# One z chunk and one o chunk of each layer as a 2x2 block product with seven products

## The chip, the core and the metric

The kernel runs on one core of a Trainium2 chip. The metric is the device time of one execution in microseconds (us). The core's engines work side by side, each from its own queue of instructions: PE (TensorE, matrix products into PSUM), DVE (VectorE, elementwise work), ACT (ScalarE, functions and copies), POOL (GpSimd) and SP (SyncE, which here only issues transfers). Semaphores hold an engine until what it needs is there.

## The reference

Two layers over 256 positions of width 2048, then a last RMSNorm. A layer normalises x, multiplies it with a wide input matrix, and splits the result: q and k (convolved), v, an output gate o, a gate z for the mLSTM heads, and xb and zb for a gated linear recurrence. Both mixers' results, each multiplied by silu of its z, go through an output matrix and are added to x.

```python
u = rms_norm(x, norm_g)
p = u @ w_in
qk, v, o, z_a, ig, fg, xb, z_b = jnp.split(p, SPLIT_AT, axis=-1)
...
h = mlstm_chunkwise(q, k, v, i_pre, log_f)
h = h * jax.nn.sigmoid(o.astype(f32)).reshape(b_, s_, H_A, DV_A)
...
y_a = h.astype(x.dtype) * jax.nn.silu(z_a)
...
y_b = rg_lru(xc.astype(f32), w_a, b_a, w_x, b_x, lam).astype(x.dtype) * jax.nn.silu(z_b)
return x + jnp.concatenate([y_a, y_b], axis=-1) @ w_out
```

All is float32. o and z are 2048 columns wide each; the kernel works them off in four chunks of 512 columns.

## The kernel before

**Units and halves.** A layer has four groups g of two heads and 512 channels. A group's input chunks are o, qk, v, xb, z and zb, 512 columns each, 2048 rows deep. The weights lie in memory as units of 128 x 2048 numbers (1 MB); a chunk is four units, a unit two halves. One half carries two row blocks of 128 rows; it is multiplied with both halves of the positions (two times 128), and each product is made of three: a float32 number is split into a rounded part H and a remainder L, and H*H, H*L and L*H are added up in PSUM. That makes 12 matmuls of 128x512 for a half (`mm_a`, line 315). The activations x are kept split as well, transposed, 128 rows a block (`x_s`).

**Splitting the weights.** A unit is loaded by SP into one of three buffers `raw` (`load_unit`, 259). `prepare` (286) splits a half: ACT casts it to wH (line 308), DVE subtracts to get wL (309; it shows as line 168, that of a helper). There are four pairs of buffers wH/wL. The main loop (1101) issues, for half n, first the split of half n + 3 (AHEAD), then the half's matmuls, then what follows them.

**The work behind a chunk.** When a chunk's last half is done, a post function takes its result out of PSUM: `o_post` (sigmoid), `v_post`, `qk_post` and `xb_post` (both swap to channel order over DRAM and back, then convolve; the names are tok, blk, moved, fr, ch), `z_post`, `zb_post`. The longer ones put a generator on the list `bg`; after each half `pump` runs these generators in order for a budget (1.05 us by their own estimates, or 2.6 when more than two are in the list). Where a step needs a key that isn't there yet, `require` runs the generators until it is. So the order in which instructions are issued comes from this loop; each engine's final order is made by the framework's scheduler, by that order and by when operands are ready. Lines made by hand with `order` fix single places.

**The sequence.** In group 0 it is o, qk, v, xb, zb, z, gate; in group 2, o, v, qk, then two output chunks of group 1, xb, two output chunks, z, gate, zb. A gate unit (`gate_half`, 739) makes the recurrence's two gates: 48 matmuls of 128x256 (line 753) into four banks ps_gt, each emptied by two sigmoids (758). It requires xb's convolution (`gate_before`, 873). Behind it `gate_post` (763) has ACT make exponentials (770), tanh (776) and a square root, and DVE the recurrence.

**PSUM.** The eight banks are two accumulators acc of two banks, and four auxiliary banks (two names, two buffers each; `aux`, 99) for ps_gt, ps_S, ps_n and a few others. The output chunks of groups 0 to 2 go through a buffer `stage` (891), from which POOL adds them to x in DRAM.

## Time and profile before

| what | us |
|---|---|
| median of the runs (1493.61 to 1494.64) | 1493.76 |
| span of the profiled execution, first to last instruction | 1491.3 |
| PE busy | 1481.6 |
| PE weight loads busy | 1241.1 |
| DVE busy | 1050.9 |
| ACT busy | 925.8 |
| POOL busy | 81.8 |

Moved in all are 345.66 MB, 232 GB/s on the mean. The profile comes from one execution; its durations are those of that execution, and what lies around the span (the start and the end of the program) is not in it. In the rows of the groups "xN" counts instructions, then come busy time in us, mean ns of one, and the idle time of the engine just ahead of them with what ended it. The chain of work that ended last is followed back from the last instruction, at each step to what released it.

### The profile page before, as it was taken

Reading aid. Unit: us, or ns where it says so; the run is one execution under the profiler, and the core shown is the slowest. Engines: PE = TensorE matmul, PEld = TensorE weight load, DVE = VectorE, ACT = ScalarE, POOL = GpSimd, SP = SyncE. Lnnn points to the kernel's source line nnn. Section 1 sums busy time; section 2 is a strip of 40 time slices with the busy share of each in tenths; the row PEclk is TensorE's granted clock in tenths of the full one; section 3 lists DMA queues with packets and bytes.
Section 4 is the critical chain, followed back from the end, with each engine's and each line's share of the span. In section 5 each row is a group of like instructions: output and inputs, shape, how many; then the busy total and the mean of one; then the engine's idle time right before and its main releaser. Section 6 shows DMA issues by size and latency. Waiting matters only on the chain.

```text
span 1491.3 us, 18541 instructions
## 1 busy us (share of the span) xinstructions
PE 1481.6 (99%) x6894; PEld 1241.1 (83%) x6894; DVE 1050.9 (70%) x1406; ACT 925.8 (62%) x1167; POOL 81.8 (5%) x154
## 2 busy tenths in 40 slices
PE   9999999999999999999999999999999999999997
PEld 8888888888888888888888888888888888888886
DVE  6778976675567855778867798765855678556785
ACT  7656864575565855658575667645755567555675
POOL 0010100000000000000000101000000000000002
PEclk9999999999999999999999999999999999999999
DMA  9866766866677666876886666568666777577783
GB/s 337 296 224 221 227 221 208 254 224 216 199 239 232 217 225 217 258 258 226 270 277 195 231 219 240 205 205 253 223 223 216 238 223 234 200 229 265 231 282 111
DMA packets 91370, 345.66 MB, mean 232 GB/s; under 512 B 9984, under 2 KB 30480, under 8 KB 69776
## 3 DMA queue, kind: packets, MB, share of 16 engines
q1 hardware_dynamic: 79472, 306.44, 60.2%
q0 software_dynamic: 9344, 33.58, 9.1%
q10 hardware_dynamic: 2464, 4.47, 0.8%
q8 instruction: 54, 0.88, 0.2%
q14 instruction: 36, 0.29, 0.0%
HBM read 307.20 MB, written 37.24 MB: 231 GB/s over the span
## 4 chain that ended last, share of the span: by engine, by line
PE 99%; ACT 0%; DVE 0%; issue 0%; ACTq 0%
PE acc L332 89%; PE ps_gt L753 3%; PE acc L345 1%; PE acc L995 1%; PE acc L994 1%; PE acc L996 1%; PE acc_x L995 0%; PE acc_x L994 0%; PE acc_x L996 0%; PE ps_blank L110 0%; PE ps_n L589 0%; PE ps_n L587 0%; PE ps_n L588 0%; PE ps_g L500 0%; PE ps_g L503 0%; PE ps_S L588 0%
## 5 line engine op out<-in xcount | busy, mean ns | idle before, releaser
L332 PE MATMUL acc<-wH,x_s 128*128 128x512 f32 x3008 | 930.0, 389 | 0.0
L168 DVE TENSOR_TENSOR wL<-raw,wH 128x1024 fp32r<-128x1024 f32 (+1 forms) x532 | 636.5, 1204 | 341.8 <-ACT wH L308 341.3
L308 ACT CAST wH<-raw 128x1024 fp32r<-128x1024 f32 (+1 forms) x532 | 548.0, 1037 | 398.5 <-PE acc L332 367.6
L332 PEld LDWEIGHTS acc<-wH,x_s 128*128 128x128 f32 x3008 | 564.6, 188 | 116.9
L332 PE MATMUL acc<-wL,x_s 128*128 128x512 f32 x1504 | 583.9, 389 | 0.0
L332 PEld LDWEIGHTS acc<-wL,x_s 128*128 128x128 f32 x1504 | 282.3, 188 | 58.1
L332 PE MATMUL acc<-wH,yaH 128*128 128x512 f32 x224 | 87.4, 390 | 0.0
L332 PE MATMUL acc<-wH,ybL 128*128 128x512 f32 x224 | 87.3, 390 | 0.0
L332 PE MATMUL acc<-wH,yaL 128*128 128x512 f32 x224 | 87.2, 389 | 0.0
L332 PE MATMUL acc<-wL,ybH 128*128 128x512 f32 x224 | 87.2, 389 | 0.0
L332 PE MATMUL acc<-wH,ybH 128*128 128x512 f32 x224 | 87.2, 389 | 0.0
L332 PE MATMUL acc<-wL,yaH 128*128 128x512 f32 x224 | 87.2, 389 | 0.0
L332 PEld LDWEIGHTS acc<-wH,ybL 128*128 128x128 f32 x224 | 42.0, 188 | 9.1 <-DVE ybL L168 0.3
L332 PEld LDWEIGHTS acc<-wH,yaL 128*128 128x128 f32 x224 | 42.1, 188 | 9.0
L332 PEld LDWEIGHTS acc<-wH,ybH 128*128 128x128 f32 x224 | 42.1, 188 | 8.5
L332 PEld LDWEIGHTS acc<-wL,ybH 128*128 128x128 f32 x224 | 42.0, 188 | 8.5
L332 PEld LDWEIGHTS acc<-wL,yaH 128*128 128x128 f32 x224 | 42.1, 188 | 8.4
L332 PEld LDWEIGHTS acc<-wH,yaH 128*128 128x128 f32 x224 | 42.0, 188 | 8.2
L446 DVE STREAM_TRANSPOSE blk<-tok 128x1024 f32<-128x1024 f32 x33 | 40.8, 1237 | 11.0 <-ACT tok L436 11.0
L436 ACT ACTIVATE tok<-acc,rstd 128x512 f32<-128x512 f32 x46 | 29.1, 684 | 30.6 <-PE acc L332 30.6
L450 POOL DMA_DIRECT2D fr<-moved x34 | 18.9, 556 | 506.5 <-DMA moved<-blk 260.1
L892 ACT COPY stage<-acc 128x1024 f32<-128x1024 f32 x24 | 24.4, 1017 | 35.5 <-PE acc L332 35.3
(209 smaller groups left out, 1308.5 us busy)
## 6 DMA issues: line engine op xcount, KB each, us to landing
raw<-in_ws_dram SPq DMA_DIRECT2D x168, 1024.0 KB, 5.1
raw<-in_ws_dram SPq DMA_DIRECT2D x190, 512.0 KB, 4.9
fr<-moved POOLq DMA_DIRECT2D x34, 512.0 KB, 6.0
moved<-blk SPq DMA_DIRECT2D x132, 128.0 KB, 2.6
x_d<-stage POOLq DMA_DIRECT2D x24, 512.0 KB, 5.4
x_d<-x_acc ACTq DMA_DIRECT2D x8, 512.0 KB, 8.4
x_acc<-x_d SPq DMA_DIRECT2D x8, 512.0 KB, 4.4
xp<-in_xt_dram SPq DMA_DIRECT2D x8, 256.0 KB, 7.2
```

The lines of the kernel that those rows point to most:

```text
L168: return V.tensor_tensor(out=o, in0=a, in1=b, op=op)
L308: st["wH"] = S.copy(out=H[:, o], in_=r[:, o])
L332: st["mm"] = PE.matmul(o, a_[:, kt, P * t : P * t + P], W[:, k], start=b, stop=z)
L345: PE.matmul(ps[:, ct, T * part : 2 * T], W[:, k, P * ct : P * ct + P], moving, start=first and k == 0 and part == 0, stop=last and k == 3 ...
L436: S.activation(out=by_block(tok, t), in_=acc[:, t, :].rearrange("p (c m j) -> p c m j", c=4, m=4), func=AF.Copy, scale=rstd[:, t : t + 1])
L446: V.transpose(out=blk.rearrange("p m n -> p (m n)"), in_=tok.rearrange("p m c t j -> p (m c t j)"))
L450: back.dma_start(out=fr.rearrange("p a c t i -> p a (c t i)"), in_=moved)
L753: PE.matmul(o, W[:, ib, jl], xs[:, ib, a, :], start=j == 0 and i == 0 and W is Hv and a == 0, stop=i == 1 and W is Lv, skip_group_check=True)
L892: S.copy(out=stage, in_=ps)
L994: PE.matmul(o, yH[:, kt, tsl], Hv[:, k, cs], start=start and k == 0, stop=False)
L995: PE.matmul(o, yH[:, kt, tsl], Lv[:, k, cs], start=False, stop=False)
L996: PE.matmul(o, yL[:, kt, tsl], Hv[:, k, cs], start=False, stop=stop and k == 1)
```

## The change

The z chunk of group 2 and the o chunk of group 3 (`PAIR`) leave the sequence. With x as 2x2 blocks (two halves of the positions, two halves of the 2048 rows) and the weights as 2x2 blocks (two halves of the rows, two chunks), the product of both is made from seven block products in place of eight, each from sums or differences of blocks (the scheme known as Strassen's in Winograd's form).

- `block_halves` gives 28 halves as 14 pairs per layer: four phases of 4, 4, 2 and 4 pairs, two products at a time (one at a time in the third), in the two new PSUM banks bank0 and bank1. Such a half has two row blocks but only one half of the positions: 6 matmuls. Where a product needs a sum of weight blocks, DVE adds the raw blocks ahead of the split, 4, 12, 0 and 4 times in the four phases.
- A pair loads one unit of two pieces of 512 KB; a pair of the second phase two.
- `block_sums`, a generator, makes the four sums S1 to S4 of x blocks and their H and L parts, in buffers that share their place with x_acc (now two tiles, xa0 and xa1).
- The 14 pairs are spread evenly from the v chunk of group 0 to the place of z in group 2, directly ahead of that group's gate.
- After each phase the banks are emptied into `res`; after the last the results go to `o_post` and `z_post` (o from a generator that waits for group 2's recurrence, with the sign turned).
- The auxiliary banks have one buffer each (two in place of four).
- Smaller: nb goes into E, Pt shares the place of ch, the gate weights have one buffer; qk's generator waits for o's sigmoid too; the first output chunk of group 2 requires it ahead of its use of `stage`.

```diff
+PAIR = (("z", NG - 2), ("o", NG - 1))
...
     def aux(name):
         st["aux"] = 1 - st["aux"]
-        return psum.tile([P, 512], F32, tag=f"aux{st['aux']}", name=name, bufs=2)
+        return psum.tile([P, 512], F32, tag=f"aux{st['aux']}", name=name)
+
+    def bank(i, name):
+        return psum.tile([P, 512], F32, tag=f"bank{i}", name=name)
...
+        elif "pieces" in ld:
+            for i, (u, o) in enumerate(ld["pieces"]):
+                nc.sync.dma_start(out=raw[:, 1024 * i : 1024 * i + 1024], in_=ws[u][:, o : o + 1024])
...
+        if "sum" in hf:
+            r = hf["sum"]()
...
-        nb = small.tile([P, 2, T], F32, tag="nb", name="nb", bufs=1)
+        E = small.tile([P, 2, 384], F32, tag="E", name="E", bufs=1)
...
-            while ("E", l, g) not in st or ("v", l, g) not in st:
+            while any((k, l, g) not in st for k in ("E", "v", "so")):
...
+                if g == NG - 2 and c == 0:
+                    require(("so", l, g + 1))
...
+    def block_sums(l):
+        sums = st["sums", l] = [act.tile([P, 2, 8, P], F32R, tag=f"xa{i}", name=f"sums{i}") for i in range(2)]
...
+        def made(i, key, terms):
+            to = sums[i]
+            for k in (0, 4):
+                ks = slice(k, k + 4)
+                two = [work.tile([P, 4, P], F32, tag=tag, name="sum_t") for tag in ("tok", "blk")]
+                for a in range(2):
+                    terms(two, a, k, ks)
+                tt_(two[0], two[0], two[1], ALU.add)
+                S.copy(out=to[:, 0, ks], in_=two[0])
+                tt_(to[:, 1, ks], two[0], to.bitcast(F32)[:, 0, ks], ALU.subtract)
+                yield 2.4
+            st[key, l] = True
...
+    def block_halves(l):
...
+                for k in range(2):
+                    aH, aL = A(2 * kp + k)
+                    s_, e_ = kp == 0 and k == 0, kp == k_last and k == 1
+                    PE.matmul(box[b], aH, Hv[:, k], start=s_, stop=False)
+                    PE.matmul(box[b], aH, Lv[:, k], start=False, stop=False)
+                    PE.matmul(box[b], aL, Hv[:, k], start=False, stop=e_)
...
+        def after4():
+            r = st["res", l]
+            top = act.tile([P, 2, 512], F32, tag="stage", name="top")
+            tt_(top[:, 0], r[:, 2], box[0], ALU.add)
+            add(r[:, 1], box[1])
+            add(r[:, 2], box[1])
...
+            bg.append(gen())
+            z_post(l, g0, r)
+
+        pairs = []
+        for kp in range(4):
+            u = load(piece(0, 0, kp), piece(0, 1, kp))
+            pairs.append([half([u], lambda u=u: half_of(u, 0), plain(0, 0), 0, kp),
+                          half([u], lambda u=u: add(half_of(u, 1), half_of(u, 0)), summed(0), 1, kp, "S1",
+                               after=after1 if kp == 3 else None)])
+        for kp in range(4):
+            u, w = load(piece(0, 0, kp), piece(0, 1, kp)), load(piece(1, 1, kp), piece(1, 0, kp))
+            pairs.append([half([u, w], lambda u=u, w=w: add(half_of(w, 0), add(half_of(u, 1), half_of(u, 0))),
+                               summed(1), 0, kp, "S2"),
+                          half([w], lambda w=w: add(half_of(w, 1), half_of(w, 0)), plain(1, 1), 1, kp,
+                               after=after2 if kp == 3 else None)])
...
+    for l in reversed(range(DEPTH)):
+        a, b = span[l]
+        pairs = block_halves(l)
+        for i in reversed(range(len(pairs))):
+            at = a + (i + 1) * (b - a) // len(pairs)
+            order_[at:at] = pairs[i]
...
-            while st["nload"] < len(order_) // 2 and st["nload"] <= (nprep + 5) // 2:
-                load_unit(order_[2 * st["nload"]])
+            while st["nload"] < len(loads) and (st["nload"] < 3 or loads[st["nload"] - 3]["last"] < nprep):
+                load_unit(loads[st["nload"]])
```

More of the change, by code (lines that the diff above doesn't have):

```diff
@@ L157, in tile_trunk @@
     gbs = const.tile([NH, DEPTH, 2], F32, name="gbs")
-    gwr = [small.tile([P, KT, 16], F32, tag="gwr", name=f"gwr{l}") for l in range(DEPTH)]
+    gwr = []
     ident = const.tile([P, P], F32, name="ident")
@@ L276, in load_unit, with half_of @@
         else:
-            nc.sync.dma_start(out=raw, in_=ws[blocks[item, j]])
+            nc.sync.dma_start(out=raw, in_=ws[blocks[ld["at"]]])
         if 3 <= n < 7:
             load_x(n - 3)
+    def half_of(ld, i):
+        return ld["raw"].rearrange("p (i n) -> p i n", i=4)[:, 2 * i : 2 * i + 2, :]
     def add_unit(mms, before=None, after=None, paired=False, own=None):
-        box = {}
-        halves.append([dict(box=box, i=i, mm=mms[i], split=None, paired=paired, own=own and own[i],
+        ld = {"paired": paired}
+        halves.append([dict(loads=[ld], i=i, mm=mms[i], split=None, paired=paired, own=own and own[i],
                             before=before if i == 0 else None, after=after if i == 1 else None) for i in range(2)])
@@ L302, in prepare @@
             L = wsp.tile([P, 2, 512], F32R, tag="L", name="wL")
-        opening = n < 4
+        opening = n < 4 and "sum" not in hf
         for j, o in enumerate((slice(0, 1), slice(1, 2)) if opening else (slice(0, 2),)):
@@ L385, in rms_stats @@
         st["rstd", l] = rstd
+        neg = small.tile([P, 2], F32, tag="neg", name="neg")
+        ts_(neg, rstd, -1.0, ALU.mult)
+        st["neg", l] = neg
     def rms_bcast(l):
@@ L589, in mm3, with o_post @@
         PE.matmul(o, aL, bH, start=False, stop=last)
-    def o_post(l, g, acc):
+    def o_post(l, g, acc, sign="rstd"):
         if g > 0:
@@ L931, in out_chunk, with part, s1, s2 @@
             add_unit(mms, before=lambda k=ready: require(k), after=postfn if half_src == 1 else None)
+    def block_sums(l):
+        sums = st["sums", l] = [act.tile([P, 2, 8, P], F32R, tag=f"xa{i}", name=f"sums{i}") for i in range(2)]
+        x_ = st["x"]
+        def part(r, c, a, k):
+            return x_.bitcast(F32)[:, 8 * c + k : 8 * c + k + 4, a, P * r : P * r + P]
+        def made(i, key, terms):
[10 more added lines that the diff above has]
+            st[key, l] = True
+        def s1(two, a, k, ks):
+            tt_(two[a], part(1, 1, a, k), part(1, 0, a, k), ALU.subtract)
+        def s2(two, a, k, ks):
+            stt(two[a], sums[0].bitcast(F32)[:, a, ks], -1.0, part(0, 0, a, k), ALU.mult, ALU.subtract)
+        def s3(two, a, k, ks):
+            tt_(two[a], part(0, 0, a, k), part(1, 0, a, k), ALU.subtract)
+        def s4(two, a, k, ks):
+            stt(two[a], sums[1].bitcast(F32)[:, a, ks], -1.0, part(0, 1, a, k), ALU.mult, ALU.subtract)
+        yield from made(0, "S1", s1)
+        yield from made(1, "S2", s2)
+        while ("phase", l, 0) not in st:
+            yield "wait"
+        yield from made(0, "S3", s3)
+        while ("phase", l, 1) not in st:
+            yield "wait"
+        yield from made(1, "S4", s4)
```

131 lines of the change are left out of this document (104 added, 27 removed).

## The prediction

> **What bounds the kernel now.** First the page: busy times, the chain that ended last, the costliest groups.
>
> ```profile
> span 1491.3 us, 18541 instructions
> PE 1481.6 (99%) x6894; PEld 1241.1 (83%) x6894; DVE 1050.9 (70%) x1406; ACT 925.8 (62%) x1167; POOL 81.8 (5%) x154
> ...
> PE 99%; ACT 0%; DVE 0%; issue 0%; ACTq 0%
> ```
>
> TensorE (PE) is the whole chain. VectorE (DVE) at 70% and ScalarE (ACT) at 62% only feed it. So a matmul taken out is worth its full spacing, as long as the feeders stay ahead. The spacing comes from the chain in order of time, where uninterrupted pieces have their counts:
>
> ```profile
> 145.56 5.60 PE ps_gt L753 x48
> 151.16 65.30 PE acc L332 x288
> ```
> ```profile
> 312.71 130.59 PE acc L332 x576
> ```
> ```profile
> 490.41 5.60 PE ps_gt L753 x48
> ```
>
> 130.59 / 576 = 0.2267 us for each 128x512 product, though one is listed with 0.389 us (they are pipelined). A half of a unit, 12 products, lasts 2.72 us. The feeders, from the groups by line:
>
> ```profile
> L168 DVE TENSOR_TENSOR wL<-raw,wH 128x1024 fp32r<-128x1024 f32 (+1 forms) x532 | 636.5, 1204 | 341.8 <-ACT wH L308 341.3
> L308 ACT CAST wH<-raw 128x1024 fp32r<-128x1024 f32 (+1 forms) x532 | 548.0, 1037 | 398.5 <-PE acc L332 367.6 <-DMA raw<-in_ws_dram 15.5 <-ACT wH L308 4.0
> ```
>
> ACT's splits wait mostly for PE to free a weight buffer (367.6 us), hardly ever for a load (15.5): usually the splits run as far ahead as their four buffers let them. "Usually" is the word the rest hangs on.
>
> **Part by part.** *Removed.* Two chunks of a layer cost 16 row blocks x 2 token halves x 3 products x 2 = 192 matmuls; seven block products of 8 x 3 cost 168. 24 fewer in each of two layers: 48 x 0.2267 = **10.9 us** off PE. The new stationaries are 128x128 like the old, so I keep the spacing.
>
> *Added for the feeders.* Rows for the sizes (512 elements, and 1024 from SBUF):
>
> ```profile
> L168 DVE TENSOR_TENSOR xcs<-xc,xcs 128x512 fp32r<-128x512 f32 x16 | 10.9, 678 | 0.0
> L733 ACT CAST xcs<-xc 128x512 fp32r<-128x512 f32 x16 | 9.9, 620 | 7.9 <-DVE xc L171 5.4 <-DVE dn L671 2.4
> L168 DVE TENSOR_TENSOR qc<-qc,qsg 128x1024 f32<-128x1024 f32 x8 | 9.8, 1221 | 4.8 <-ACT qsg L629 4.8
> ```
>
> Per layer 28 short halves take the place of 16 long ones, each with a split as large as before: 12 more, 14.4 us DVE and 12.4 us ACT. Weight blocks are added 4 + 12 + 0 + 4 = 20 times, 24.4 us DVE. The activation sums are 8 steps of 4 DVE operations (21.7 us) and an ACT copy (5.0). Emptying the two banks is 7 DVE operations of about 0.69 (4.8) and two copies (1.2). Together 65 us DVE and 19 us ACT per layer: DVE goes to 1051 + 131 = 1182 us, 80% of the span. The busy times by stretch say where:
>
> ```profile
> 70.00:97.20 27.20, 27.20 (x122) 22.53 (x121) 23.04 (x39) 16.33 (x20) 6.48 (x15) 1.00 0.59 191
> 151.60:178.80 27.20, 27.20 (x122) 22.51 (x121) 24.89 (x26) 25.07 (x35) 0.64 (x2) 1.00 0.64 218
> ```
> ```profile
> 70.00:505.00 435.00, 435.00 (x2033) 364.66 (x2032) 310.61 (x426) 270.11 (x330) 25.67 (x48) 1.00 0.69 224
> ```
>
> (columns: stretch, length, PE, weight loads, DVE, ACT, POOL, clock, DMA share, GB/s). In the part of layer 0 where the 14 pairs go, DVE grows from 311 of 435 us to about 385 of 451 (85%; 8 of the 16 halves lost lie in it): it fits on the mean. Between two pairs stand ten halves, 27 us, in which DVE has some 8 us free; the dearest pair (second phase: three additions, two splits, 6.1 us against 2.72 us of PE) needs 3.4 of them. I cost these at nothing wherever the lead is full. That lead is about 5.9 us: a buffer is freed 8.2 us (three halves) before its next use, and cast and subtraction take 2.3. If the cover is gone, each pair costs its excess, 0.9 to 3.4 us.
>
> *Where the lead is thin.* Right behind the gate of group 0:
>
> ```profile
> 147.71 1.56 ACT L758 ACTIVATE gate<-ps_gt,pars 128x256 f32<-128x256 f32 x4
> ...
> 152.06 1.28 ACT L770 ACT_TABLE_LOAD   x1
> 153.35 1.71 ACT L770 ACTIVATE Dt<-gate,sp 128x256 f32<-128x256 f32 x4
> 154.97 1.70 ACT L776 ACTIVATE gate<-gate,sp 128x256 f32<-128x256 f32 x4
> 156.57 1.99 ACT L308 CAST wH<-raw 128x1024 fp32r<-128x1024 f32 x2
> ```
> ```profile
> 157.84 2.35 DVE L168 TENSOR_TENSOR wL<-raw,wH 128x1024 fp32r<-128x1024 f32 x2
> ...
> 163.11 1.22 DVE L168 TENSOR_TENSOR wL<-raw,wH 128x1024 fp32r<-128x1024 f32 x1
> ```
>
> After the gate ACT works 4.6 us on exponentials ahead of the next casts. The first of the two parts wL at 157.84 is ready at 159.0 and belongs to the fourth half behind the gate, which starts at 151.16 + 3 x 2.72 = 159.3: a lead of 0.3 us. The third pair stands exactly there, as third and fourth half. Two short halves bring the need for the fourth forward to 158.0 (its first product needs wH alone, so wL at 158.2): PE waits 0.8. The part after next is ready at 164.3; PE, now at 159.0 + 1.1 + 2.72 = 162.8, wants it at 163.1: 1.2 more. So **2.0 us per layer, 4.0 together**; below, 0 if the scheduler moves casts ahead of the exponentials, above 7 if the pair's whole DVE work (3.6 each) falls on PE. I take 4.0, straight from the rows.
>
> *Auxiliary banks.* Four become two, so the third of a gate's four groups of products, due 24 x 5.60/48 = 2.80 us after the gate's start (148.36), must wait for both sigmoids of the first.
>
> ```profile
> L758 ACT ACTIVATE gate<-ps_gt,pars 128x256 f32<-128x256 f32 x64 | 26.3, 490 | 2.0 <-PE ps_gt L753 2.0
> ```
>
> Four in 1.56 us, 0.49 each, start 0.36 apart; the second ends at 147.71 + 0.36 + 0.49 = 148.56. That is 0.2 late, I put 0.4 with the hand-over, times 8 gates: 0 to 3.2 us. An order that puts other ready products there hides it; I take the middle, 1.6. Elsewhere the banks are used halves apart.
>
> *The gate of group 2.* The last pair stands directly ahead of it, where eight halves of z stood. The conv of xb, which this gate requires, now has 8 long and 2 short halves plus 2.4 us of ps_n products from the end of xb: 26.9 us, where it had 47 (443.3 to 490.4). What it took:
>
> ```profile
> 443.33 1.27 ACT L436 ACTIVATE tok<-acc,rstd 128x512 f32<-128x512 f32 x2 [1.67 <-PE acc L332]
> ```
> ```profile
> 457.49 1.05 ACT L470 COPY ch<-fr 128x1024 f32<-128x1024 f32 x1
> ```
> ```profile
> 475.14 0.68 DVE L168 TENSOR_TENSOR xcs<-xc,xcs 128x512 fp32r<-128x512 f32 x1
> ```
> ```profile
> 856.74 1.66 DVE L171 SCALAR_TENSOR_TENSOR xc<-ch,pars,xc 128x255 f32<-128x255 f32 x4
> ```
>
> Ready 32.5 us after the end of xb: 5.6 too late, if nothing changed. But the qk work that lay between its operations now comes four halves earlier, 11 us. ch lands 14.2 us after the end of xb, as before; with its copy (1.05) and a first ACT step (0.6) DVE can begin at 15.9. What it then must do is 12 conv steps (four in 1.66 us, so 0.4 apart: 4.8), two subtractions (1.4), four splits and one addition (6.0): 12.2 us in 11.0, with the last subtraction needed only 1.4 later. I take 0.5 per layer, 1.0 together, with 0 and 11.2 as ends. The first result goes into the stage buffer, which a transfer has just left:
>
> ```profile
> L892 ACT COPY stage<-acc 128x1024 f32<-128x1024 f32 x24 | 24.4, 1017 | 35.5 <-PE acc L332 35.3
> ```
> ```profile
> x_d<-stage POOLq DMA_DIRECT2D x24, 512.0 KB, 5.4
> ```
>
> Copied from 2.72 us before the pair's end on, 1.0 for the copy, 0.3 to the issue, 5.4 to the landing: free 4.0 us after the pair. Behind that wait stand on DVE the other results and the next splits.
>
> *Moved.* z's two sigmoids (ACT), its products (DVE) and the channel swap (four DMAs on SP, one on POOL) come right behind the last pair, ahead of the gate's casts as before; o's two sigmoids of group 3 now wait for the scan of group 2, and only qk's ps_n products of group 3 need them, tens of us later. Nothing.
>
> *Sums S1, S2 in group 0.* They put 10.8 us on DVE between 72 and 105 us of layer 0, ahead of the splits that are issued later.
>
> ```profile
> 74.00 1.06 ACT L308 CAST wH<-raw 128x1024 fp32r<-128x1024 f32 x1 [0.17 <-PE acc L332]
> ```
> ```profile
> 86.84 1.01 DVE L176 TENSOR_SCALAR E<-nb,at 128x256 f32<-128x256 f32 x4 [3.80 <-DMA nb<-nG_d]
> ```
>
> At 74.0 a cast still waits for PE, so the lead is full (5.9), and DVE is idle for 3.8 us: 10.8 - 5.9 - 3.8 = 1.1 left, which conv steps of the same stretch, issued later, can make room for: 0 to 3, I take 0.
>
> *Loads.* 10 MB more per layer, as 512 KB pieces on SP's queue:
>
> ```profile
> raw<-in_ws_dram SPq DMA_DIRECT2D x168, 1024.0 KB, 5.1
> raw<-in_ws_dram SPq DMA_DIRECT2D x190, 512.0 KB, 4.9
> ```
>
> A second-phase pair needs two loads; the second is freed two halves before its use (5.4 us) against 5 us of landing, with the split's lead behind it. Nothing; with the DMA share at 0.69 rising to 0.74, 1 us each for 8 pairs if it is late. POOL's queue gains only the wait of its broadcast for the E buffer, free since the last group.
>
> Sum: 4.0 + 1.6 + 1.0 = 6.6 given back of 10.9; the span goes to 1487.0. The median of the runs, 1493.76, lies 2.5 us above the span of the profiled execution, and I keep that: **1489.5 us**.
>
> **The rivals.** *A, full gain* (0.20): the order is made anew and the waits are filled; 1483 to 1486. For it: PE never waits today in spite of leads of 0.3. Against it: the thin stretch is filled by ACT, which no order shortens.
>
> *B, VectorE falls behind* (0.18): S1 to S4 and the dear pairs eat the lead in several places, 0.9 to 3.4 us for some five pairs in a layer; about 8 us on top of the gate waits: 1494 to 1498. For it: stretches at 92% now. Against it: full leads through most of groups 1 and 2.
>
> *C, slower: the gate of group 2 idles PE* (0.22). The conv steps are issued behind the last pair's results; if DVE's order puts them behind the write into the stage buffer, free only 4.0 us after the pair, then 4.0 + 3 x 0.6 for the results + 2 conv steps (2.4) + two subtractions (1.2) = 9.4 us per layer. It decides from 5.4 us per layer, the gain of a layer. With 18.8 in place of 1.0: 1507; half of it: 1498.
>
> The clock that was granted is full all along; the only slow products, 619 ns against 279 for the same size in a gate, stand at the very start:
>
> ```profile
> core 0: 1491.3 us, clock 0.998
> ```
> ```profile
> L110 PE MATMUL ps_blank<-blank 128*128 128x256 f32 x14 | 6.0, 619 | 1.3 <-DVE blank L108 1.3
> ```
> ```profile
> L753 PE MATMUL ps_gt<-xcs,wH 128*128 128x256 f32 x256 | 45.2, 279 | 0.0
> ```
>
> The Trainium skill, page "TensorE: Matmul & The Clock Gate", section "What's actually happening", says that an idle window of about 3.4 us puts the array back to half clock until it has been busy for one again. By it each idling of case C would cost an estimated 1.7 us more, 3.4 in all, and 1507 would be about 1510; no row here shows a stop in the middle.
>
> *D, the change is not what it says* (0.03): another spacing of the short halves; 5% slower products on 336 matmuls are 4 us, 1494.
>
> **How the numbers follow.** Forecast (0.37): 1486 to 1492.5. About 0.2% (3 us) is what a measurement of this kernel can tell from no change. Below 1490.8: A's 0.20, three quarters of the forecast (0.28), 0.02 of C and D = 0.50. Within: the forecast's rest 0.09, 0.08 of B, 0.07 of C and D (a small idling) = 0.24. Slower: 0.10 of B and 0.16 of C = 0.26. The range runs from 1483, the whole gain, to 1500, which leaves out the upper half of C.
>
> **What would show it.** Right: about 6846 matmuls; 168 block products per layer at 0.227; waits of PE only in pieces of about 1 us behind the gate of group 0 and inside gates; DVE near 1180 us. Step wrong: no wait behind group 0's gate (A); waits for wL spread over groups 0 and 1 (B); a gap of over 5 us ahead of gate products of group 2 (C). The forecast is wrong if the lead of the splits, today 0.3 at its thinnest, breaks in places where I counted it full.

## The result, and the profile after

| | median us (runs) | span | products | DVE busy | ACT busy |
|---|---|---|---|---|---|
| before | 1493.68 (1493.08 to 1494.64) | 1491.3 | 6894 | 1050.9 | 925.8 |
| after | 1542.16 (1537.83 to 1543.86) | 1536.1 | 6846 | 1166.6 | 953.8 |

The changed kernel is slower: ratio 1.0318, 95% interval 1.0306 to 1.0330. That is 48.5 us more, where 4 less were forecast, and it lies 42 us above the end of the range. The profile after is that of the fastest of the four runs (1537.83), so its span grew by 45 us, not by 48.5.

The page of the changed kernel, the lines that answer to those of before (busy times; then the chain that ended last, by engine and by line):

```profile
PE 1489.2 (97%) x6846; PEld 1233.3 (80%) x6846; DVE 1166.6 (76%) x1550; ACT 953.8 (62%) x1208; POOL 89.6 (6%) x154
...
PE 32%; DVE 5%; DMA 4%; ACT 2%; issue 1%; SPq 0%; DVEq 0%; ACTq 0%; POOLq 0%
```

PE is no longer the whole chain: DVE and transfers are in it (what is listed of the chain begins 851 us into the program, so its shares do not add up to 100%). DVE's load is what was counted on, 1167 against 1182. On the mean it still has a quarter of its time free, and yet PE waits. The waits of PE, from the changed kernel's list (engine, line, waited for: us in all, times, longest):

```profile
PE acc L359 <- DVE wL L186: 20.5, 14, 2.9
PE ps_n L618 <- DVE dn L189: 6.3, 2, 3.3
PE ps_b L1031 <- ACT wH L335: 3.0, 2, 1.5
PE acc L359 <- ACT wH L335: 2.2, 5, 0.7
PE ps_b L1032 <- DVE wL L186: 2.2, 3, 0.9
PE ps_gt L784 <- ACT xcs L764: 1.9, 2, 1.0
```

Before, this list had a single row, at the very start of the program. Most of it now is waiting for a split. Counted over the starts of all 6846 products, PE loses 54 us above the plain spacing (3 before). 54 - 3 less the matmuls saved, 11, is 40 of the span's 45. The groups show the feeders' side:

```profile
L335 ACT CAST wH<-raw 128x1024 fp32r<-128x1024 f32 (+1 forms) x556 | 569.7, 1036 | 390.7 <-PE acc L359 293.6 <-DMA raw<-in_ws_dram 35.8 <-DVE raw L186 31.5
...
L186 DVE TENSOR_TENSOR raw<-raw 128x1024 f32<-128x1024 f32 x40 | 48.8, 1219 | 18.9 <-DMA raw<-in_ws_dram 18.6
```

ACT's casts waited 367.6 us for PE before and 293.6 now; in its place they wait for loads (35.8 us, 15.5 before) and for DVE's additions (31.5). That is a sign of a smaller lead, though no measure of it: kernels further down that are faster than this one have less of this wait too. The 40 additions of weight blocks cost what was assumed, 1.22 us each; DVE also stands 18.6 us in front of them, waiting for a load, with the splits queued behind.

### The profile page after: what moved, and what is told of

It is laid out like the page before. It is cut to its first block, busy times and chain, and to the rows that moved or that the text cites. A ratio compares the mean times of both kernels' runs of the same rounds, so it can differ in the third digit from the quotient of the medians.

```text
span 1536.1 us, 18833 instructions
## 1 busy us (share of the span) xinstructions
PE 1489.2 (97%) x6846; PEld 1233.3 (80%) x6846; DVE 1166.6 (76%) x1550; ACT 953.8 (62%) x1208; POOL 89.6 (6%) x154
## 5 line engine op out<-in xcount | busy, mean ns | idle before, releaser
L359 PE MATMUL acc<-wH,x_s 128*128 128x512 f32 x2752 | 858.2, 390 | 2.2 <-ACT wH L335 2.2
L186 DVE TENSOR_TENSOR wL<-raw,wH 128x1024 fp32r<-128x1024 f32 (+1 forms) x556 | 662.8, 1204 | 238.4 <-ACT wH L335 236.6
L335 ACT CAST wH<-raw 128x1024 fp32r<-128x1024 f32 (+1 forms) x556 | 569.7, 1036 | 390.7 <-PE acc L359 293.6
L359 PEld LDWEIGHTS acc<-wH,x_s 128*128 128x128 f32 x2752 | 517.6, 188 | 111.4 <-ACT wH L335 4.6
L359 PE MATMUL acc<-wL,x_s 128*128 128x512 f32 x1376 | 537.6, 392 | 19.9 <-DVE wL L186 19.7
L359 PEld LDWEIGHTS acc<-wL,x_s 128*128 128x128 f32 x1376 | 259.0, 188 | 79.6 <-DVE wL L186 26.9
L186 DVE TENSOR_TENSOR raw<-raw 128x1024 f32<-128x1024 f32 x40 | 48.8, 1219 | 18.9 <-DMA raw<-in_ws_dram 18.6
L784 PE MATMUL ps_gt<-xcs,wH 128*128 128x256 f32 x256 | 48.3, 287 | 2.3 <-ACT xcs L764 1.9
```

What stands on the lines that cost most here:

```text
L186: return V.tensor_tensor(out=o, in0=a, in1=b, op=op)
L335: st["wH"] = S.copy(out=H[:, o], in_=r[:, o])
L359: st["mm"] = PE.matmul(o, a_[:, kt, P * t : P * t + P], W[:, k], start=b, stop=z)
L784: PE.matmul(o, W[:, ib, jl], xs[:, ib, a, :], start=j == 0 and i == 0 and W is Hv and a == 0, stop=i == 1 and W is Lv, skip_group_check=True)
```

## The experiments

Eighteen kernels, each beside the kernel before on the same chip (its medians there lie between 1493.35 and 1493.63). A difference between two of them of 2 or 3 us is no more than their intervals leave open.

| run | what it is | median us | ratio to before, 95% interval |
|---|---|---|---|
| e13_fewer | before, 48 products less | 1482.13 | 0.9923 (0.9908 to 0.9938) |
| e6_small_moves | before, small moves | 1494.86 | 1.0009 (0.9999 to 1.0018) |
| e1_two_banks | before, two banks | 1507.47 | 1.0094 (1.0079 to 1.0109) |
| e5_later_h1 | e1, ps_n later | 1498.85 | 1.0037 (1.0024 to 1.0050) |
| e10_no_load | e7, pairs without loads | 1514.74 | 1.0143 (1.0127 to 1.0158) |
| e16_singles | e10, pairs set apart | 1513.85 | 1.0133 (1.0118 to 1.0148) |
| e7_one_load | e4, no second load | 1515.85 | 1.0152 (1.0137 to 1.0167) |
| e14_tiny_second | e4, second load of 8 KB | 1518.74 | 1.0165 (1.0148 to 1.0182) |
| e12_long_halves | e7, products twice | 1568.19 | 1.0499 (1.0483 to 1.0515) |
| e4_neither | after, no additions, no sums | 1529.63 | 1.0229 (1.0209 to 1.0250) |
| e2_no_wadd | after, no weight additions | 1526.81 | 1.0220 (1.0205 to 1.0236) |
| e3_no_sums | after, no activation sums | 1538.82 | 1.0299 (1.0277 to 1.0321) |
| e18_one_load_adds | after, no second load | 1524.10 | 1.0206 (1.0191 to 1.0221) |
| e11_later_h1 | after, ps_n later | 1532.35 | 1.0260 (1.0245 to 1.0275) |
| e9_moved_pool | after, swap on POOL's queue | 1573.53 | 1.0532 (1.0514 to 1.0549) |
| e8_later_pairs | after, pairs in groups 1 to 3 | 1538.92 | 1.0302 (1.0285 to 1.0319) |
| e15_placed | e11, pairs placed by hand | 1561.11 | 1.0449 (1.0434 to 1.0465) |
| e17_off_gates | e11, two pairs moved | 1532.96 | 1.0255 (1.0238 to 1.0273) |

### Were the 10.9 us there?

```diff
+                if k < less:
+                    turns = turns[:2] + turns[3:] if k == 0 else turns[:1] + turns[2:]
...
+                            2 - i if (kind, g) in (("z", NG - 2), ("o", NG - 1)) else 0) for i in range(2)]
```

> The kernel before with 48 products left out and nothing else: 12 of the 96 products of z of group 2 and 12 of o of group 3, in each layer, so the output is not the reference's. The prediction's first term: 48 x 0.2267 = 10.9 us less, 1482 to 1484. Rival, the freed time is given back as waits for splits, since eight halves last 2.27 or 2.49 us in place of 2.72: 1485 or above.

11.5 us less (1493.63 to 1482.13), and PE's starts show no wait that was not there before. The first term was right: a product is worth its full spacing, here 11.5 / 48 = 0.24 us in the time (10.9 / 48 in PE's busy time, 1481.6 to 1470.7). Everything that follows is therefore to be explained from 1482, not from 1494.

### The banks

```diff
-        return psum.tile([P, 512], F32, tag=f"aux{st['aux']}", name=name, bufs=2)
+        return psum.tile([P, 512], F32, tag=f"aux{st['aux']}", name=name)
...
```

> The kernel before with one part of the change alone: the auxiliary PSUM banks cut from four to two (the last chunk takes the two freed ones). Theory 1, VectorE's new work and the loads behind it eat the lead of the splits: two banks by themselves cost what the prediction took for the gates, 0 to 3 us, so 1494 to 1497. Theory 2, the banks cost the time: the waits before ps_n and ps_gt of the changed kernel (3.17 and 3.52 ahead of ps_n, about 8 ahead of the gates of group 2) come back here, 10 us or more, so 1504 or above.

1507.47, 14.1 us more than before, with not one block product in it: the rival. The timeline of e1_two_banks in layer 1 (start, us, engine, line, instruction):

```profile
876.97 0.39 PE L335 MATMUL acc<-wH,x_s 128*128 128x512 f32 x1
...
878.75 0.15 DVE L174 SCALAR_TENSOR_TENSOR dn<-ps_n,at 128x1 f32<-128x1 f32 x1
...
879.47 1.22 DVE L171 TENSOR_TENSOR wL<-raw,wH 128x1024 fp32r<-128x1024 f32 x1
880.60 0.48 DVE L174 SCALAR_TENSOR_TENSOR hh<-ps_n,dn,so 128x256 f32<-128x256 f32 x1
...
881.23 0.55 PE L590 MATMUL ps_n<-vH,PH 128*128 128x258 f32 x1 [3.87 <-DVE dn L171]
```

ps_n takes one bank for each half of the positions. With four banks the second head has two of its own; with two it must wait for the first head's to be emptied, and that is four small DVE steps for each bank (three on dn, then hh) with a split and steps on E between them. The first bank comes free at 881.08, with hh (the profile names the dn step that ends just behind it), and PE has stood since 877.2. So I let the second head's products be issued later:

```diff
             for h in range(2):
+                for _ in range(2 * h):
+                    yield "wait"
                 pns = [aux("ps_n") for _ in range(2)]
```

> The kernel before with two auxiliary banks, as in e1_two_banks (1507.47), and one thing more: the second head's ps_n products are issued two steps of the background work later. Theory, the wait ahead of ps_n is for VectorE to empty the two banks of the first head: the stalls of 2.60 and 4.03 us at 128 and 877 go, and the time falls by 5 to 7 us, to 1500 to 1502.5. Rival, the wait is only pushed to the next user of a bank: 1506 to 1509.

> The changed kernel with the second head's ps_n products issued two steps of the background work later, as in e5_later_h1. Theory, the banks' part is the same wait as there: the stalls ahead of ps_n (3.17 at 259 and 3.52 at 1021, 1.2 more) go, 6 to 9 us less, 1533 to 1536. Rival, behind the pairs VectorE is late in any case and the stall comes at the next wL: 1539 to 1543.

Alone, 8.6 us come back (1498.85), in the changed kernel 9.8 (1532.35), both more than expected. So this wait is shown, in both kernels. (In e1_two_banks the waits for ps_n are 6.6 us; right behind the longer one PE's clock is at half for 3.41 us, which costs another 1.6, as the last section works out, and e5_later_h1 has no such stretch.) Of the 14.1 us 5.5 remain, and in e5_later_h1 PE's only waits of over 0.4 us in the groups' work stand behind the gate of group 0 (1.23 us in each layer, and 0.53 in one). I put them down to the gates, but not as forecast, as waits of PE: ACT waits there. Before, its sigmoids stood 2.0 us for ps_gt (the row in the prediction); in e1_two_banks:

```profile
ACT gate L761 <- PE ps_gt L756: 10.0, 8, 1.3
```

That is 8 us more, about 1 us for each of the eight gates. Behind the gate of group 0, where the lead is 0.3 and the exponentials follow, such a delay reaches PE; behind the others PE has no wait of over 0.4 us. No run frees the gates' banks alone, so this last part is read from the rows, not shown.

### The small moves

```diff
-        st["nb", l, g] = nc.gpsimd.dma_start(out=nb.rearrange("p h t -> p (h t)"), in_=src)
+        st["nb", l, g] = nc.gpsimd.dma_start(out=E[:, :, 0:T], in_=src.rearrange("p (h t) -> p h t", h=2))
...
```

> The kernel before with the small moves of the change alone: the broadcast of the gates lands in E itself, Pt takes the buffer of ch, and qk's tail waits for o's sigmoids; four auxiliary banks. Theory of the prediction: nothing, 1493 to 1495. Rival, the later broadcast (its wait on VectorE is 13.7 us in the changed kernel, 6.0 before) and the shared buffer delay VectorE: 1496 to 1502.

Pt in ch's buffer and the wait for so are taken from the change likewise; the single buffer of the gate weights and the halves of x_acc are not. 1494.86 against 1493.61, a term of 1.3 us, with an interval (0.9999 to 1.0018, that is -0.1 to 2.7 us) that just takes in no difference.

### Additions and sums

```diff
-                          half([u], lambda u=u: add(half_of(u, 1), half_of(u, 0)), summed(0), 1, kp, "S1",
+                          half([u], lambda u=u: half_of(u, 1), summed(0), 1, kp, "S1",
...
-            bg.append(block_sums(l))
+            st["S1", l] = st["S2", l] = st["S3", l] = st["S4", l] = True
```

(The first edit is one of four in e2_no_wadd; the second is in e3_no_sums, where the products take plain blocks of x; e4_neither has both.)

> The changed kernel without its additions of weight blocks: each combined half uses one loaded block as it is, so the output is not the reference's. All loads, splits, activation sums and products stay. 40 additions of 1.22 us (49 us of VectorE) go. Theory 1: PE's 54 us above the plain spacing fall by half or more, 1505 to 1517. Theory 2 (banks): less than 5 us go, 1537 or above. Theory 3, late loads alone: nothing goes but what the freed buffers bring, 1530 to 1540.

> The changed kernel without the activation sums S1 to S4: the combined products take plain blocks of x, so the output is not the reference's. Weight additions, loads and splits stay. 64 operations of VectorE, about 43 us, and 16 copies go. Theory 1: the stalls in the stretches where the sums stand (2.4 and 3.5 us at 100 to 106 and 859 to 868, 3.7 and 3.4 at 314 to 319 and 1078 to 1082) go, 10 to 20 us, 1522 to 1532. Theory 2: within 3 us of 1542.

> The changed kernel without weight additions and without activation sums: only the halved units, the extra loads, the two banks and the moved steps are left, so the output is not the reference's. Theory 1: nearly all waits go, the 10.9 us of matmuls taken out show, 1483 to 1495. Theory 2: banks and moved steps keep 20 us or more, 1505 or above.

Theory 1 falls in all three. Without weight additions 15.4 us come back (1526.81, in none of the three ranges), without sums 3.3, without both 12.5, though 80 us of DVE are gone (1166.6 to 1086.2). 47 us above 1482 remain in a kernel whose DVE is busy little more than before (1050.9). What the two kinds of work cost does not add up (15.4 and 3.3 against 12.5). The intervals of e2_no_wadd and e4_neither overlap, so it isn't shown that leaving out the sums as well makes anything worse; but the profiles show where a gain can go. PE's waits for ps_n are 7.3 us in e4_neither against 3.3 in e2_no_wadd, and its clock is at half for five windows of 3.41 us against none (the last section tells what such a window is and costs).

### The loads

```diff
-            u, w = load(piece(0, 0, kp), piece(0, 1, kp)), load(piece(1, 1, kp), piece(1, 0, kp))
+            w = load(piece(1, 1, kp), piece(1, 0, kp))
...
+                m = 8 if ld.get("tiny") else 1024
+                nc.sync.dma_start(out=raw[:, 1024 * i : 1024 * i + m], in_=ws[u][:, o : o + m])
```

(The first edit, on e4_neither, gives e7_one_load, and on the changed kernel e18_one_load_adds; the second, on e4_neither, e14_tiny_second.)

> e4_neither (1529.63: no additions, no activation sums, output not the reference's) with the second load of the four second-phase pairs gone as well, 4 MB per layer less. Theory L, loads come late because a pair turns over its three raw buffers in half the time: ACT's waits for raw (68.3 us over 37 casts in e4_neither) fall and the time by 5 to 15 us, 1515 to 1525. Theory S, the lead of the splits is itself halved at a pair (two short halves give four buffers of splits 2.7 us less of PE to hide behind) and loads don't matter: 1527 to 1530.

> e4_neither (1529.63) with the first of the two loads of a second-phase pair cut from 1 MB to 8 KB: its buffer is taken, its two transfers stand in SP's queue at the same place, a tiny copy reads it, only the bytes are gone; the output is not the reference's. e7_one_load without that load took 1515.85. Theory T, the transfer itself is late (5.7 us for a piece, in a time of 5.4): 1515 to 1519. Theory B, buffers and queue: a pair uses up two of the three, and the next load waits for the pair's last subtraction: 1526 to 1530.

> The changed kernel (1542.16) with the first load of each second-phase pair gone, 8 MB in all, and every addition, split and activation sum kept (the additions take the blocks of the other load, so the output is not the reference's). Theory T, the bytes are late there as in e4_neither against e7_one_load: 11 to 16 us less, 1526 to 1531. Rival, beside the additions the transfer is hidden, VectorE being later still: 1538 to 1543.

Eight loads of 1 MB, costed at nothing, cost 13.8 us in the bare kernel (e4_neither against e7_one_load) and 18.1 in the full one (1542.16 to 1524.10), more than the theory's 11 to 16. With the buffer taken and the place in SP's queue kept, but the bytes gone, 10.9 of the 13.8 come back: it is mostly the transfer (theory T), and less the buffers and the queue. The changed kernel around a second-phase pair, by stretches of 4 us (busy PE, granted clock, DMA share, GB/s):

```profile
302.00:306.00 4.00, 4.00 (x20) 1.00 0.91 350
306.00:310.00 4.00, 4.00 (x19) 1.00 1.03 415
310.00:314.00 4.00, 4.00 (x19) 1.00 1.01 239
314.00:318.00 4.00, 3.48 (x16) 1.00 0.45 115
318.00:322.00 4.00, 1.17 (x6) 1.00 0.41 172
```

and its timeline there:

```profile
312.19 1.05 ACT L500 COPY ch<-fr 128x1024 f32<-128x1024 f32 x1 [3.08 <-DMA fr<-moved]
...
315.37 4.81 DVE L189 SCALAR_TENSOR_TENSOR xc<-ch,pars,xc 128x255 f32<-128x255 f32 x12
320.09 1.22 DVE L186 TENSOR_TENSOR wL<-raw,wH 128x1024 fp32r<-128x1024 f32 x1
```

The DMA engines are full from 302 to 314. A pair of this phase asks for 2 MB in the 2.72 us of its products, 770 GB/s, where 415 is the most that these rows show. What comes late is not the load alone: the channel swap is in flight at the same time. From issue to landing, its last transfer (fr, 512 KB) takes 9.1 us here, against a median of 5.3 for all such transfers of this kernel and 7.3 at this place in e18_one_load_adds; the four ahead of it (moved) take 4.4 to 4.7 us each, against 2.1 to 2.4 there. ACT waits 3.08 us for fr, and then DVE does the 12 steps of the convolution in one go, 4.81 us, with the next split behind them. PE stands 3.0 us. In e18_one_load_adds the copy waits for nothing and the steps are spread out (12 as 7, 4 and 1):

```profile
303.85 1.05 ACT L500 COPY ch<-fr 128x1024 f32<-128x1024 f32 x1
...
307.02 2.85 DVE L189 SCALAR_TENSOR_TENSOR xc<-ch,pars,xc 128x255 f32<-128x255 f32 x7
309.78 1.22 DVE L186 TENSOR_TENSOR wL<-raw,wH 128x1024 fp32r<-128x1024 f32 x1
```

PE has no wait there, though the engines are full in that kernel too, for some 8 us. With the second loads gone, PE's waits for ps_n fall as well, from 6.9 us to 0.6: late loads make DVE late, and the banks with it, so this price and that of the banks overlap. The Trainium skill, page "DMA: Bandwidth & Descriptors", section "Specifications", gives 435 GB/s as the ceiling of the fabric into SBUF; the 415 above, and 423 in e4_neither, stop just under it.

SP's queue was another suspect: loads stand in it behind moved<-blk, which waits for DVE.

```diff
-            nc.sync.dma_start(out=moved[:, a].rearrange("(m j) n -> j m n", m=4), in_=blk[32 * a : 32 * a + 32])
+            nc.gpsimd.dma_start(out=moved[:, a].rearrange("(m j) n -> j m n", m=4), in_=blk[32 * a : 32 * a + 32])
```

> The changed kernel with one line other: the four transfers moved<-blk of each channel swap are issued from POOL's queue, not SP's, so that no load of weights stands behind one that waits for VectorE. Theory Q, this blocking is what makes the second loads late (in e4_neither SP issued nothing from 290.3 to 295.2 and ACT then waited 7.1 us): 8 to 20 us come back, 1522 to 1534. Rival, the buffers of raw, not the queue, hold the loads back: 1538 to 1545, or slower where POOL's own waits delay the swap.

1573.53, 31 us worse. The list of waits of e9_moved_pool has

```profile
POOL moved L479 <- DVE blk L476: 555.0, 29, 60.1
```

so POOL's queue now stands where SP's stood, the swaps come later, and waits elsewhere grew (PE's clock is also at half for 15 windows, against four). This says that the swap must not be late; it does not clear SP's queue of a share, nor convict it.

### The short halves

```diff
-            pairs.append([half([u], lambda u=u: half_of(u, 0), plain(0, 0), 0, kp),
+            pairs.append([half([], lambda: xraw(0), plain(0, 0), 0, kp),
...
-                for k in range(2):
+                for k in (0, 1, 0, 1):
...
-            order_[at:at] = pairs[i]
+            m = at + 5 * (i < 13)
+            order_[m:m] = pairs[i][1:]
+            order_[at:at] = pairs[i][:1]
```

(The first edit is that of e10_no_load, xraw being a piece of x; the second that of e12_long_halves, the third that of e16_singles.)

> e7_one_load (1515.85) with no loads at all for the pairs: each short half splits a piece of x of the same size, so it has the same casts, subtractions and products, but the output is not the reference's. Theory L, a pair's own loads make it late: the 18 us that e7_one_load lies above 1498 (1482.6 for the products, 14.1 for the banks in e1_two_banks, 1.3 for the moves in e6_small_moves) go, 1497 to 1503. Theory S, the lead of the splits is halved by short halves, whatever they load: 1511 to 1517.

> e7_one_load (1515.85) with each short half's six products issued twice, so that a half lasts 2.72 us like any other; the output is not the reference's. 336 products more are 76.2 us of PE (336 x 0.2267): 1592 if shortness has no part in the waits. Theory S or L, a short half turns over its buffers in half the time, and the 18 us above 1498 come from that: 1572 to 1578.

> e10_no_load (1514.74, no loads for the pairs, output not the reference's) with the two short halves of a pair set five halves apart, the last pair left as it is. Theory S, the lead at a pair is three halves less two short ones, 5.4 us less 2.3 for cast and subtraction, and one short half alone leaves 6.8 less 2.3: the waits fall by half or more, 1500 to 1507. Rival, the waits come from what ACT and VectorE have to do around the gates and not from the pairing: 1512 to 1517.

1514.74 with no loads for the pairs at all: the pairs' remaining loads cost 1.1 us in all (1515.85 to 1514.74), which the intervals don't tell from nothing, and the 17 us above 1497.5 (1482.13 + 14.1 + 1.3) are due to what is left: casts, subtractions and products of short halves, the emptying of their banks, and the new order. 1568.19 with every product twice, that is 1492 after the 76.2 us of added products are taken off, and less than the 1572 to 1578 that were expected: with the halves as long as the others the 18 us are gone, and 5.5 of the banks' part with them. The waits of PE in e12_long_halves,

```profile
PE acc L359 <- DVE wL L186: 2.7, 3, 1.6
...
PE ps_n L618 <- DVE hh L189: 0.6, 2, 0.5
```

against e10_no_load:

```profile
PE acc L359 <- DVE wL L186: 10.6, 12, 1.2
PE ps_b L1034 <- ACT wH L335: 3.0, 2, 1.5
PE acc L359 <- ACT wH L335: 2.8, 7, 0.6
PE ps_n L618 <- DVE hh L189: 2.6, 2, 2.4
```

So shortness is what costs: a half still takes 1.04 us of ACT and 1.22 of DVE for its split, but covers 1.36 us with products in place of 2.72, so that of that time DVE has 0.14 us left for all else, where a long half leaves 1.50. My picture of how, two short halves side by side that halve the lead for a moment, fell: set five halves apart they cost the same (1513.85), and it is the rival, that ACT and DVE have too much to do around the gates, whose range holds. PE's waits in e10_no_load stand at the same few places in both layers, most of them by gates: in pieces of over 0.4 us, 4.4 us a layer behind the gate of group 0 (of which e1_two_banks has 1.8 too), 2.8 around the gate of group 2 and 2.1 some 25 us behind it, 2.5 ahead of ps_n, and 1.1 or 1.2 in group 0. What the traces show there is a reserve that is not made good. In e10_no_load, in two stretches behind the gate of group 2 (PE, weight loads, DVE, ACT, POOL):

```profile
526.00:540.00 14.00, 14.00 (x76) 11.73 (x76) 9.09 (x10) 12.70 (x23) 0.56 (x1) 1.00 0.56 172
540.00:550.00 10.00, 8.25 (x35) 6.25 (x34) 9.90 (x13) 9.97 (x14) 0.00 (x0) 1.00 0.58 206
```

In the second ACT and DVE are busy without a break while PE waits. In the kernel before, behind the same gate:

```profile
488.00:502.00 14.00, 14.00 (x87) 12.54 (x85) 10.40 (x11) 13.34 (x23) 0.19 (x1) 1.00 0.61 188
502.00:516.00 14.00, 14.00 (x63) 11.62 (x62) 13.27 (x12) 12.14 (x16) 0.38 (x1) 1.00 0.76 268
```

ACT has 13.34 of 14 us, then DVE 13.27 of 14, and PE never waits: the full lead carries it over 28 us. After a pair the lead is less, and it is not filled again before such a stretch. That this is the cause for all pairs is argued from these rows, not shown: the last pair's results, emptied by DVE at the same place, are work that the kernel before has in another form, and no run takes them away alone.

### The places

```diff
-        if item[:2] + item[2:] == ("in", item[1], "v", 0):
+        if item[0] == "in" and item[2:] == ("qk", 1) and j == 0:
...
-            at = a + (i + 1) * (b - a) // len(pairs)
+            at = span[l] + (8 + 8 * i if i < 6 else 65 + 7 * (i - 6) if i < 13 else 122)
...
-            at = a + (i + 1) * (b - a) // len(pairs)
+            at = a + (i + 1) * (b - a) // len(pairs) + {2: 6, 13: 6}.get(i, 0)
```

(The start of the stretch in e8_later_pairs and e15_placed, then the places of e15_placed and of e17_off_gates.)

> The changed kernel with its 14 pairs spread from the start of group 1 to the first eight halves of group 3 in place of group 0 to the end of group 2; all work is done. Theory P, the places count (group 0, behind its gate, ahead of the gate of group 2): the stalls at 100 to 106, 167 to 181, 525 to 530 and their like in layer 1, some 22 us, go, 1518 to 1526. Theory S, each pair costs wherever it stands: 1536 to 1548.

> e11_later_h1 (1532.35, all work done) with the 14 pairs put by hand: the first eight halves behind the gate of group 0, then 7 or 8 apart through groups 1 and 2, none within seven halves behind the gate of group 1 or directly ahead of the gate of group 2, the last eight halves behind it. Theory P, part of the waits is due to thin places (behind the gate of group 0, ahead of the gate of group 2): 1518 to 1526. Theory S, short halves cost wherever they stand: 1529 to 1535. By neither does it come down to the kernel before.

> e11_later_h1 (1532.35, all work done) with two of the 14 pairs moved: the third, behind the gate of group 0, six halves later, and the last, directly ahead of the gate of group 2, six halves later, which is four behind that gate. Theory P, the waits by these two gates (4.5 and 4.0 us behind the first, 3.8 and 6.0 around the second, 2.4 and 2.4 behind it) belong to the pairs beside them: 12 to 20 us less, 1512 to 1520. Rival, ACT and VectorE have the same to do there and the pair takes its waits along: 1528 to 1535.

e8_later_pairs took 3.2 us less than the changed kernel, with a loss of its own in it: z's result comes so late that PE stands 5.6 us in each layer ahead of the output chunks of group 3. Without these 11 us it would lie near 1528, between the two theories. But behind each of these two waits PE's clock is at half for 6.83 us, which is worth some 3.2 us more each (the last section has the price). Without those too the run would lie near 1521, inside theory P's range, so it does not speak against P. Placing by hand lost 29 us against e11_later_h1. PE's clock is at half for 13 windows of 3.41 us in it, against four, which is up to 14 of the 29; the largest part of the waits is in this row (2.6 us in e11_later_h1), where the products of second-phase pairs wait for casts that come late:

```profile
PE ps_b L1033 <- ACT wH L335: 21.5, 12, 3.9
```

Moving only the two pairs by the gates changed nothing (1532.96 against 1532.35). The waits at the old places went for the most part (behind the gate of group 0 about 2.5 us a layer stayed), new ones of 1.32, 0.72 and 0.55 us came beside the third pair's new place, and of 2.38 and 3.30 behind the last's. Theory P fell in e15_placed and e17_off_gates. For the two pairs of e17_off_gates the rival is shown: the pairs take their waits along. For the other twelve the runs leave it open.

## Why the prediction failed, step by step

| step, as the prediction put it | forecast us | measured us | by |
|---|---|---|---|
| removed: 48 x 0.2267 | -10.9 | -11.5 | e13 |
| auxiliary banks | +1.6 | +14.1 | e1 |
| small moves ("nothing") | 0 | +1.3 | e6 |
| short halves: lead behind group 0's gate 4.0, gate of group 2 1.0, elsewhere nothing | +5.0 | +18.4 | e7, from 1497.5 |
| second loads ("Nothing") | 0 | +13.8 | e4 less e7 |
| additions and sums ("at nothing wherever the lead is full") | 0 | +12.5 | after less e4 |
| sum | -4.3 | +48.6 | measured in all: +48.5 |

The first three rows were each measured alone on the kernel before, the last two are differences between kernels, and the row of the short halves is what is left between them. So the rows add up by the way they are made, which proves nothing, and that row holds all that the change moves and no run tested alone. Another order would divide them otherwise (the second loads alone are 18.1, and e12 shows that short halves and banks share 5.5). Four steps failed, the banks, the short halves, the second loads and the additions, each by about 12 to 14 us.

- **Removed.** Right.
- **Banks.** The step that failed is the sentence "Elsewhere the banks are used halves apart". It looked at when the products are issued, not at how long a bank stays taken: ps_n's banks are held until DVE gets to hh, over 4 us. 8.6 of the 14.1 are there. For the gates, priced at 1.6, the place of the wait was wrong too: PE hardly waited inside gates (one wait of 0.3 us in the changed kernel), ACT did.
- **The thin lead behind group 0's gate.** Right as a place: PE waits there in both layers, in pieces of 0.7 to 1.7 us, 4.9 and 3.5 in all against 2.0 each. Part of it is the banks' (1.8 each in e1_two_banks).
- **The gate of group 2.** xb's convolution was late by 1.9 us in both layers together (the row ps_gt <- xcs), against 1.0: the mechanism, at twice the size. Case C's wait for the stage buffer came as well, and the sum had nothing for it. The convolution was ahead of the write, not behind it, so the first gate products did not wait for it, but the next split did (changed kernel, layer 0; then PE's answer):

```profile
525.05 2.36 DVE L186 TENSOR_TENSOR wL<-raw,wH 128x1024 fp32r<-128x1024 f32 x2
529.61 0.69 DVE L186 TENSOR_TENSOR top<-res,ps_b 128x512 f32<-128x512 f32 x1 [2.20 <-DMA x_d<-stage]
530.21 1.28 DVE L186 TENSOR_TENSOR res<-res,ps_b 128x512 f32<-128x512 f32 x2
531.40 1.22 DVE L186 TENSOR_TENSOR wL<-raw,wH 128x1024 fp32r<-128x1024 f32 x1
```
```profile
532.68 0.50 PE L359 MATMUL acc<-wL,x_s 128*128 128x512 f32 x1 [2.04 <-DVE wL L186]
```

DVE stands 2.20 us here and 2.25 in layer 1, and PE 2.2 and 2.3 us: some 4.5 us from start to start in all, in place of C's 18.8.

- **The lead.** The step behind two of the four rows, short halves and additions, is "That lead is about 5.9 us", used as a fixed stock that a pair may draw on and that is full again at the next one. It is three halves of products less 2.3 us, so every short half takes 1.36 us of it, and the next stretch with ACT or DVE full finds it smaller; that the halves' shortness costs the 18 us is shown by e12_long_halves, the way through the lead is argued. The mean (85%) said that all would fit; the two stretches of the prediction's own view, DVE at 23 to 25 of 27 us, pointed at two of the places (waits at 100 to 106 and 167 to 181), though not at those at 259, 315 to 321 and 526 to 533.
- **Loads.** Priced at their landing time, 5 us against 5.4, one at a time. The rate was not worked out: 2 MB in 2.72 us. The end of the range, 1 us each for eight, was below the 1.7 to 2.3 measured.
- **Rivals.** B had the right sign and kind (waits for wL spread over groups 0 and 1) with a price of 8 us; C had the right sign and, with the stage buffer, a wait that came at a quarter of its price. That the result is slower by so much was in none of them: none put these together, since each term was bounded by itself with full leads around it.

## What to carry over

Where the bound engine lives on a lead, an edit that shortens its instructions while the feeders' work for each stays the same must be priced as a loss of lead, and the lead followed from one crowded stretch to the next; a mean over 400 us cannot show it. A buffer's price is how long its last reader takes to come, not how often it is written. And a load that is added is worked out as a rate, bytes over the time in which they are wanted, next to the highest rate that the trace has seen.

## What was unexpected in the hardware

PE's clock drops to half for 3.41 us at a time in the middle of the changed kernel, four times, and no wait ahead of them is that long by itself but one (3.52 us). Windows of the changed kernel (length, PE busy with the products started, granted clock, DMA share, GB/s):

```profile
926.50:929.90 3.40, 3.12 (x14) 1.00 0.31 79
929.90:933.30 3.40, 1.69 (x5) 0.99 0.47 154
933.30:936.70 3.40, 3.40 (x10) 0.51 0.82 276
936.70:940.10 3.40, 3.40 (x17) 1.00 0.39 110
```

A window in which 5 products start, where 15 fit, is followed by one at half clock. The slow stretches start at whole multiples of 3.413 us from one another, so the chip seems to judge fixed windows: in all traces of this study (56 slow stretches between a kernel's start and its end, 12 of them two windows long) the window ahead had PE stand for 2.05 us or more of its 3.41, in pieces that may be short, counted from the starts of the products, and full-speed windows in which it stood for up to 2.02 us were not followed by one. A wait of 3.17 us that lay across two windows (259, ahead of ps_n) cost no clock. The prediction cited the Trainium skill, page "TensorE: Matmul & The Clock Gate", section "What's actually happening", for an idle window of about 3.4 us, and estimated 1.7 us for each from it: the size of the window and that it runs free agree with these traces, but here a window only 60% idle is enough. At half clock a 128x512 product takes 0.427 us from start to start in these traces, in place of 0.2267, so that 8 fit in a window where 15 did: 1.6 us for each, about 6 us for the four, as an estimate that leaves out what the feeders gain meanwhile. Waits of PE cost more than they last. It shows in the runs of the changed kernel too: the span is 1536.1 us at a granted clock of 0.994, 1538.8 at 0.992, and 1542.1 at 0.990 and at 0.989.
